# A two-layer transformer block in fp32: every remaining block of the modulation product moved into the first attention

## The chip, the cores and the metric

The kernel runs on one core of a Trainium2 chip, in one launch. The metric is the device time of that launch in microseconds (us). Three timed runs of the kernel before gave 3011.73, 3011.78 and 3012.26 us; the median is 3011.78.

## The reference

1024 latent tokens and 256 context tokens of width 1024 pass through two layers. Each layer has a mixer and a SwiGLU feed-forward network (FFN), each behind a normalisation that is modulated: shift, scale and gate come from one linear map of a conditioning vector.

```
for i in range(2):
    m_lat = silu(c)     @ ada_w[i] + ada_b[i]      # ada_w[i]: 1024 x 6144
    m_ctx = silu(c_ctx) @ ada_w[i] + ada_b[i]
    sh1, sc1, g1, sh2, sc2, g2 = split(m_lat, 6)    # the same for m_ctx
    h = rms(x, norm1_g[i]) * (1 + sc1) + sh1
    x = x + g1 * mixer_i(h, hc)                     # layer 0: Fourier groups and windowed attention
    h = rms(x, norm2_g[i]) * (1 + sc2) + sh2        # layer 1: neighbourhood attention
    x = x + g2 * ((silu(h @ wg) * (h @ wu)) @ wd)
    # layer 0 does the same for the context tokens
```

So the modulation of layer 1 depends on nothing but the inputs, and may be computed at any time before layer 1's first normalisation.

## The kernel before

All matrices are fp32. The large products run in three passes of a rounded 11-bit type (`mm3`, lines 74 to 76: high by high, low by high, high by low), so each weight tile is loaded raw, cast to its high part on ACT (line 774) and split to its low part on DVE (line 775) before TensorE (PE) can use it.

The stages follow each other in time. First come the first quarter of the modulation and layer 0's input projection, then the Fourier groups, and then layer 0's attention. After it come the output projection, layer 0's FFN (22 tiles of the hidden width, on 512, 256 and 512 tokens), layer 1's projection, its attention, and its FFN (22 tiles, on 512 and 512 tokens).

**The modulation product.** `ada_w` of both layers is cut into 48 blocks of 256 output columns, 1 MB each: blocks 0 to 23 are layer 0's, 24 to 47 layer 1's. `ada_block` (line 115) is a generator with three steps. Step 1 loads the block through SP's queue (line 124). Step 2, the products, is eight matmuls (line 130) that put the two conditioning vectors against 8 x 128 rows, in four groups of 32 output partitions, and a copy of the four partial rows on ACT (line 133, tile `ada_rows`, one buffer). Step 3, the sums, is two small matmuls against a 0/1 matrix `sel` (line 137) that add the four partial rows and turn them into columns, and an addition of the bias on DVE (line 138). Each of steps 2 and 3 takes one PSUM tile from the pool that the place of the call names.

The 48 blocks are spread over three places. Blocks 0 to 7 run at the very start. Blocks 8 to 23 run in layer 0's attention (lines 719 to 728). Blocks 24 to 47 run in layer 0's FFN: `modulation1` (line 1009) chains them, and `gate_up` (line 843) advances the chain by two steps behind the first chunk of tokens and by one behind each of the other two, from the third tile of the hidden width on (line 866). There the block is loaded in two halves of 512 KB into the ring `w_raw` (two buffers), the ring through which the FFN's own raw weights pass (line 772).

**Layer 0's attention.** It has 80 units (10 blocks of 128 queries, 2 key heads, 4 query heads), taken in 40 pairs by `pipeline2` (line 605). In each pair PE computes the scores of two new units (lines 602, 603), turns the probabilities of the pair two back (line 592, tiles `pt_ps`, three buffers) and multiplies older ones with the values (line 692, tile `po`). DVE adds the mask and takes the maximum (line 571) and copies turned tiles (line 598), ACT takes the exponents (line 577), POOL normalises (line 583). The calls in `before` are issued ahead of a pair's scores, those in `after` behind it. The order on PE, DVE, ACT and POOL is the written one here (`manual_schedule`); SP's order, and all orders in the FFN, are set by the scheduler of the framework. Every fourth pair starts with `load_q0` (line 642), which loads the next 128 queries (`qraw`, 512 KB) and turns them with eight matmuls (line 649) into two `pt_ps` tiles.

Of the kernel before, what the change touches and what calls it, by code (L numbers as in the profile page):

```python
# [9 lines left out]
F32 = mybir.dt.float32  # L10
# [6 lines left out]
P = 128  # L17
D = 1024
KT = D // P
# [36 lines left out]
def bc(ap, axis, n):  # L56

    ap = ap.unsqueeze(axis)
    shape = list(ap.shape)
    shape[axis] = n  # L60
    return ap.broadcast_to(shape)


def build(tc, io):
    nc = tc.nc
    V, S, G, TE = nc.vector, nc.scalar, nc.gpsimd, nc.tensor
    pools = Pools(tc)

    def fl(ap):
        return ap.bitcast(F32)  # L70
# [24 lines left out]
    csil = cst.tile([P, KT, 32], F32, name="csil")  # L95
# [16 lines left out]
    def vec(l, which):  # L112
        return mod[l][:, which * KT:(which + 1) * KT, :]

    def ada_block(b, xpool, wpool, ptr, name, parts=1, tag="x8"):

        l, ct = b // 24, 2 * (b % 24)  # L120
        n = KT // parts
        ws = [xpool.tile([P, n, 256], F32, name="ada_w", tag=tag) for _ in range(parts)]
        for i, w in enumerate(ws):
            nc.sync.dma_start(w, io["ada_w"][b, :, i * n:(i + 1) * n])
        yield
        ps = ptr.tile([P, 512], F32, name=name)
        for i in range(2):
            for q in range(4):
                k = 4 * i + q
                TE.matmul(ps[32 * q:32 * q + 32, :256], csil[:, k, :], ws[k // n][:, k % n],  # L130
                          start=i == 0, stop=i == 1, tile_position=(0, 32 * q))
        rows = wpool.tile([P, 256], F32, name="ada_rows", bufs=1)
        S.copy(rows, ps[:, :256])
        yield
        ps = ptr.tile([P, 512], F32, name=name)
        for j in range(2):
            TE.matmul(ps[:, 2 * j:2 * j + 2], rows[:, j * P:(j + 1) * P], sel, start=True, stop=True)
        V.tensor_tensor(mod[l][:, ct:ct + 2, :], ps[:, 0:4].rearrange("p (j m) -> p j m", j=2),
                        bc(adab[:, l, ct:ct + 2], 2, 2), ALU.add)

    def ada_gain(l, which, i, ks=slice(0, KT)):
        V.scalar_tensor_tensor(nA[i][:, ks], vec(l, which)[:, ks], 1.0, bc(ng[:, i, ks], 2, 2), ALU.add, ALU.mult)
# [10 lines left out]
    def advance(steps, n):  # L153

        for _ in range(n):
            if next(steps, steps) is steps:
                return
# [32 lines left out]
    x8, x8_cm = pools.open("x8", bufs=5)  # L190
# [161 lines left out]
    for c in range(T // CH):  # L352
        h_hi, h_lo = hs[c]

        for u in range(CH // P):
            j = c * (CH // P) + u
            if c == 0:
                pf, pq, _ = acc0[u]
# [7 lines left out]
            if j == NT - 1:  # L366
# [8 lines left out]
                first = butterfly(0, fp, 1)  # L375
# [56 lines left out]
    pst, pst_cm = pools.open("pst", bufs=2, psum=True)  # L432
# [42 lines left out]
    for half in range(2):  # L475
# [5 lines left out]
        for gg in range(2):  # L481
# [3 lines left out]
            for i0, parts in ((0, (0, 4)), (2, (1, 2)), (4, (3,))):  # L485
                ps = pA.tile([P, 2, 2, P], F32, name="ps_a")
# [7 lines left out]
                n = len(parts)  # L494
# [5 lines left out]
            for s0, n, sgn, l0, st in ((0, 2, 1, 0, 4), (2, 3, 1, 1, 1), (2, 3, -1, 7, -1)):  # L500
                ps = pB.tile([P, 4, P], F32, name="ps_b")
# [12 lines left out]
    g = fp.tile([P, 2, 512], F32, name="fg", tag="fa")  # L514
# [6 lines left out]
    for grp in range(4):  # L521
        ch = slice(grp * P, grp * P + P)
        a_hi, a_lo = a_parts(2)
        ps = pA.tile([P, 2, 2, P], F32, name="ps_a")
# [5 lines left out]
        ps = pB.tile([P, 4, P], F32, name="ps_b")  # L530
# [74 lines left out]
    def pipeline2(units, before, after):  # L605


        n = len(units) // 2
        last = max([n + 2] + [a + 1 for a in after])
        for b in range(last):  # L610
            new, old, turned = (units[2 * i:2 * i + 2] if 0 <= i < n else [] for i in (b, b - 1, b - 2))
            if b < n:
                for i in (2 * b, 2 * b + 1):
                    for f in before.get(i, ()):
                        f()
                    units[i] = units[i]()
                new = units[2 * b:2 * b + 2]
            for u in new:
                u.scores()
            for i in range(2):  # L620
                for u in old[i:i + 1]:
                    u.normalise()
                for u in new[i:i + 1]:
                    u.maxima()
                for u in turned[i:i + 1]:
                    u.turn()
                for u in new[i:i + 1]:
                    u.exponents()
            for f in after.get(b, ()):
                f()  # L630


    aw, aw_cm = pools.open("aw", bufs=2)
    xq, xq_cm = pools.open("xq", bufs=2)
    pss, pss_cm = pools.open("pss", bufs=2, psum=True)
    pst, pst_cm = pools.open("pst", bufs=3, psum=True)
    psv, psv_cm = pools.open("psv", bufs=1, psum=True)

    units, before, after = [], {}, {}
    qst = {}  # L640

    def load_q0(j):
        qraw = xq.tile([P, 1024], F32, name="qraw")
        nc.sync.dma_start(qraw, q_d[:, j, :])
        qst[j] = []
        for g in range(2):
            ps = pst.tile([P, 512], F32, name="pt_ps")
            for i in range(4):
                TE.transpose(ps[:, i * P:(i + 1) * P], qraw[:, (2 * i + g) * P:(2 * i + g + 1) * P], ident)
            q = aw.tile([P, 512], F32R, name=f"q{g}")  # L650
            S.copy(q, ps)
            qst[j].append(q)
# [63 lines left out]
            for e in range(2):  # L716
                group0(j, g, e)

    def modulation(ada, i):

        if i % 2 == 0 and i // 2 + 1 < len(ada):
            advance(ada[i // 2 + 1], 1)
        advance(ada[i // 2], 1 + i % 2)

    ada = [ada_block(b, xq, aw, pst, "pt_ps") for b in range(8, 24)]
    advance(ada[0], 1)
    for i in range(2 * len(ada)):
        before.setdefault(2 * (2 + i), []).append(lambda i=i: modulation(ada, i))
    with tc.manual_schedule(engines={E.PE, E.DVE, E.Activation, E.Pool}):
        pipeline2(units, before, after)  # L730
    ada_gain(0, 4, 1)
    pools.close(psv_cm, pst_cm, pss_cm, xq_cm, aw_cm, kv_cm, ac_cm)


    class Dense:
# [96 lines left out]
                yield  # L832
            lows.pop(0)()

        def ffn(self, first, last, tail=None, extra=iter(())):
            l, wk, tok, chunks = self.l, self.wk, self.tok, self.chunks
            act = {}

# [4 lines left out]
            def gate_up(f, chunks, side=iter(()), mid=lambda: None, mid2=lambda: None):  # L843
                if f not in act:
                    act[f] = open_act(f)
                ws, a_hi, a_lo = act[f]
                for c0, n, v in chunks:
                    sl = slice(c0, c0 + n)
                    g_ps = self.pg.tile([P, 512], F32, name="g_ps")
                    u_ps = self.pg.tile([P, 512], F32, name="u_ps")  # L850
                    for ps, w in zip((g_ps, u_ps), ws):
                        for k in range(KT):
                            mm3(ps[:, :n], w[0][:, k], w[1][:, k], self.h_hi[:, k, sl], self.h_lo[:, k, sl],
                                k == 0, k == KT - 1)
                            if ps is u_ps and k == 3:
                                mid2()
                        if ps is g_ps:
                            sg = wk.tile([P, 512], F32, name="sg", tag="t5")
                            S.activation(sg[:, :n], g_ps[:, :n], AF.Silu)  # L859
                            mid()  # L860
                    V.tensor_tensor(sg[:, :n], sg[:, :n], u_ps[:, :n], ALU.mult)  # L861
                    S.copy(a_hi[:, sl], sg[:, :n])  # L862
                    V.tensor_tensor(a_lo[:, sl], sg[:, :n], fl(a_hi[:, sl]), ALU.subtract)  # L863
                    advance(side, 8)
                    if f > 1:
                        advance(extra, 2 if c0 == 0 else 1)

            def down(fs, chunks, final=None, wd=None, own=iter(()), side=lambda dt: None):
                wd = wd or down_weights(fs)
# [42 lines left out]
            if not tail:  # L912
# [1 line left out]
                    gate_up(f, chunks)  # L914
                down(block, chunks, last)
                return
            advance(extra, 999)

            (cx, c0, c1), follow, side = tail

# [3 lines left out]
            f = block[-1]  # L924
# [25 lines left out]
    C0, C1, CX = (0, 512, 0), (512, 512, 0), (SEQ, CTX, 1)  # L950
# [4 lines left out]
    dl = Dense(0, T, (C0, CX, C1), o_hi, o_lo, x)  # L955
# [10 lines left out]
    steps, last = itertools.chain(*own), norm2(C1, lambda i: V)  # L966
# [39 lines left out]
        if dt in (2, 4):  # L1006
            w_first.append(w_in1(2, len(w_first), eng=G))

    def modulation1():
        for b in range(24, 48):  # L1010
            yield from ada_block(b, dl.wr, dl.wk, dl.pm, "pmisc", 2, "w_raw")
            yield
        ada_gain(1, 1, 2)
        ada_gain(1, 4, 3)

    steps = dl.ffn(last, fin0, ((CX, C0, C1), norm1, first_weights), modulation1())
    w_first += [w_in1(2, 2, eng=G), w_in1(2, 3, eng=G)]
    ctx_ps = [in_ps() for _ in range(2)]
    in_proj(w_first, (8, 9), range(2), ctx_ps)
# [30 lines left out]
    for i, cc in enumerate((2, 0, 4, 1, 3, 5)):  # L1050
        ws = w_first if cc == 2 else [w_in1(cc, kk, pool=w1 if i % 2 else dl.ww) for kk in range(4)]
        for j in ((8, 9) if cc >= 2 else ()) + tuple(range(8)):
            if cc == 2 and j >= 8:
                ps = ctx_ps[j - 8]
            else:
                ps = in_ps()
# [29 lines left out]
    aw, aw_cm = pools.open("aw1", bufs=2)  # L1086
    pss, pss_cm = pools.open("pss1", bufs=2, psum=True)
    pst, pst_cm = pools.open("pst1", bufs=3, psum=True)
# [7 lines left out]
    units, before, after = [], {}, {}  # L1096
# [128 lines left out]
    dl = Dense(1, SEQ, (C0, C1), h_hi, h_lo, x, by_col=True)  # L1225
    own = norm2(C0)
    dl.out_proj(io["w_out1"], (C0,), lambda dt: nc.sync.dma_start(x[:, dt], x_d[:, dt]), (own,))
    last = norm2(C1, lambda i: V)
# [120 lines left out]
```

## Time and profile before

The profiled execution took 3008.44 us, of which 3006.6 us is the span of its instructions.

| Quantity | Value |
|---|---|
| timed runs, median | 3011.78 us |
| profiled execution, time | 3008.44 us |
| its span | 3006.6 us |
| PE busy | 2889.4 us (96%) |
| DVE busy | 1381.9 us (46%) |
| ACT busy | 876.2 us (29%) |
| DMA, mean | 89 GB/s |
| granted clock of PE, mean | 0.983 |

"Busy" counts an instruction from start to end. Matmuls overlap in the array, so their starts say more than their durations: a 512-column matmul of the three-pass product is listed with 0.39 us but the next one starts 0.23 us after it. PEclk is the share of full clock that PE was granted. "Idle before" a row, in square brackets, names what released the engine.

The stages lie at 0 to 225 us (first modulation, projection), 225 to 237 (end of the Fourier groups), 237 to 406 (layer 0's attention), 406 to 560 (output projection, normalisation), 560 to 1450 (layer 0's FFN as far as modulation runs in it), 2300 to 2960 (most of layer 1's FFN).

### The profile page before, as it was taken

To read this page: it belongs to the slowest core of one execution; us is meant where nothing else is said; L and a number is where in the kernel's file an instruction comes from. 1 tells how busy PE (TensorE), PEld (TensorE's weight loads), DVE (VectorE), ACT (ScalarE), POOL (GpSimd) and SP (SyncE) were. 2 spreads that over 40 slices of the span, in tenths; PEclk is the share of its full clock that TensorE was granted. 3 is DMA by queue.
4 is the path that set the end of the run, shared out by engine and by line. 5 is a ranking of instruction groups with operands and counts; after the bars stand their busy time and mean duration, and the time that the engine had idled before them with its cause. 6 is when DMAs were issued, how large, how long until landed. Compare 5 with 4: busy or idle time off the path is not lost.

```text
span 3006.6 us, 38166 instructions
## 1 busy us (share of the span) xinstructions
PE 2889.4 (96%) x15290; PEld 2329.1 (77%) x15290; DVE 1381.9 (46%) x2530; ACT 876.2 (29%) x1672; POOL 313.2 (10%) x442
## 2 busy tenths in 40 slices
PE   7989999999999999999989999999999999999999
PEld 5877778877777877777876788777787888888887
DVE  5776646331313332233367334366664444444446
ACT  4346643211111111111145222466643111111110
POOL 0113321000000000000031000355310000000000
PEclk9999999999999999999999999999999999999999
DMA  7234342112121122121124433877331111111111
GB/s 271 86 113 169 120 141 79 35 49 70 50 71 69 57 71 71 43 70 56 57 74 130 121 104 103 200 174 177 119 112 49 43 49 43 56 43 50 49 43 70
DMA packets 120673, 267.19 MB, mean 89 GB/s; under 512 B 9616, under 2 KB 67472, under 8 KB 116528
## 3 DMA queue, kind: packets, MB, share of 16 engines
q1 hardware_dynamic: 114368, 247.89, 26.1%
q0 software_dynamic: 1952, 8.32, 1.0%
q10 hardware_dynamic: 4176, 8.53, 0.8%
q8 instruction: 121, 1.98, 0.3%
q14 instruction: 56, 0.46, 0.1%
HBM read 223.69 MB, written 41.03 MB: 88 GB/s over the span
## 4 chain that ended last, share of the span: by engine, by line
PE 88%; DVE 5%; DMA 3%; ACT 3%; issue 1%; POOL 1%; ACTq 0%; SPq 0%; POOLq 0%; DVEq 0%
PE d_ps L74 9%; PE d_ps L75 9%; PE d_ps L76 9%; PE g_ps L74 7%; PE g_ps L76 7%; PE g_ps L75 7%; PE u_ps L75 7%; PE u_ps L76 7%; PE u_ps L74 7%; PE pt_ps L592 3%; PE po L1177 3%; PE s_ps L602 2%; PE s_ps L603 2%; PE po L692 1%; DMA w_raw<-w_in 1%
## 5 line engine op out<-in xcount | busy, mean ns | idle before, releaser
L879 DVE SCALAR_TENSOR_TENSOR x<-d_ps,mod,x 128x512 f32<-128x512 f32 (+1 forms) x400 | 347.0, 880 | 164.1 <-PE d_ps L76 164.1
L861 DVE TENSOR_TENSOR sg<-sg,u_ps 128x512 f32<-128x512 f32 (+1 forms) x110 | 69.8, 634 | 694.0 <-PE u_ps L76 694.0
L774 ACT CAST w_hi<-w_raw 128x1024 fp32r<-128x1024 f32 x188 | 195.9, 1048 | 644.2 <-PE d_ps L75 328.5
L74 PE MATMUL d_ps<-act_hi,w_hi 128*128 128x512 f32 (+1 forms) x880 | 334.9, 381 | 19.0 <-ACT w_hi L774 15.6
L775 DVE TENSOR_TENSOR w_lo<-w_raw,w_hi 128x1024 fp32r<-128x1024 f32 x184 | 224.9, 1227 | 266.7 <-ACT w_hi L774 263.2
L75 PE MATMUL d_ps<-act_lo,w_hi 128*128 128x512 f32 (+1 forms) x880 | 333.4, 379 | 1.3 <-DVE act_lo L863 1.3
L76 PE MATMUL d_ps<-act_hi,w_lo 128*128 128x512 f32 (+1 forms) x880 | 327.3, 376 | 0.0
L74 PE MATMUL g_ps<-o_hi,w_hi 128*128 128x512 f32 (+1 forms) x528 | 196.6, 372 | 18.4 <-ACT w_hi L774 18.4
L74 PEld LDWEIGHTS d_ps<-act_hi,w_hi 128*128 128x128 f32 x880 | 169.0, 192 | 55.4 <-ACT w_hi L774 16.1
L75 PEld LDWEIGHTS d_ps<-act_lo,w_hi 128*128 128x128 f32 x880 | 169.2, 192 | 33.0 <-DVE act_lo L863 1.8
L76 PEld LDWEIGHTS d_ps<-act_hi,w_lo 128*128 128x128 f32 x880 | 168.4, 191 | 32.1
L75 PE MATMUL g_ps<-o_lo,w_hi 128*128 128x512 f32 (+1 forms) x528 | 193.2, 366 | 0.0
L76 PE MATMUL g_ps<-o_hi,w_lo 128*128 128x512 f32 (+1 forms) x528 | 192.5, 365 | 0.3 <-DVE w_lo L775 0.3
L859 ACT ACTIVATE sg<-g_ps 128x512 f32<-128x512 f32 (+1 forms) x110 | 61.0, 555 | 440.8 <-PE g_ps L76 440.0
L75 PE MATMUL u_ps<-o_lo,w_hi 128*128 128x512 f32 (+1 forms) x528 | 188.8, 358 | 0.0
L74 PE MATMUL u_ps<-o_hi,w_hi 128*128 128x512 f32 (+1 forms) x528 | 188.6, 357 | 0.0
L76 PE MATMUL u_ps<-o_hi,w_lo 128*128 128x512 f32 (+1 forms) x528 | 188.5, 357 | 0.0
L583 POOL TENSOR_SCALAR pr<-pr,st 128x640 f32<-128x640 f32 (+2 forms) x208 | 156.3, 752 | 225.3 <-DVE st L582 165.6
L862 ACT CAST act_hi<-sg 128x512 fp32r<-128x512 f32 (+1 forms) x110 | 63.5, 577 | 389.5 <-DVE sg L861 389.5
L577 ACT ACTIVATE pr<-sm,st 128x640 f32<-128x640 f32 (+4 forms) x208 | 162.7, 782 | 27.7 <-POOL sm L566 18.6
L809 POOL TENSOR_TENSOR nrm_ss<-nrm_ss,nrm_sq 128x512 f32<-128x512 f32 (+1 forms) x38 | 48.2, 1269 | 1169.6 <-PE d_ps L76 1046.6
L592 PE MATMUL pt_ps<-ident,pr 128*128 128x128 f32 x944 | 139.0, 278 | 6.8 <-ACT pt L596 3.5
(266 smaller groups left out, 6010.2 us busy)
## 6 DMA issues: line engine op xcount, KB each, us to landing
ada_w<-ada_w SPq DMA_DIRECT2D x24, 1024.0 KB, 4.9
ada_w<-ada_w SPq DMA_DIRECT2D x48, 512.0 KB, 4.0
w_raw<-w_gate SPq DMA_DIRECT2D x44, 512.0 KB, 3.2
w_raw<-w_up SPq DMA_DIRECT2D x44, 512.0 KB, 3.2
w_raw<-w_down SPq DMA_DIRECT2D x44, 512.0 KB, 3.3
k<-k_d SPq DMA_DIRECT2D x28, 640.0 KB, 10.1
w_raw<-w_out SPq DMA_DIRECT2D x32, 512.0 KB, 3.3
w_raw<-w_in SPq DMA_DIRECT2D x24, 512.0 KB, 4.1
```

What stands on the lines that cost most here:

```text
L74: TE.matmul(out, lh, rh, start=first, stop=False)
L75: TE.matmul(out, lh, rl, start=False, stop=False)
L76: TE.matmul(out, ll, rh, start=False, stop=last)
L577: S.activation(self.pr[:, :n], self.sm[:, :n], AF.Exp, bias=st[:, 0:1], scale=-1.0, accum_out=st[:, 1:2])
L583: G.tensor_scalar(self.pr[:, :n], self.pr[:, :n], st[:, 3:4], 0.0, ALU.mult, ALU.add)
L592: TE.transpose(pt[:, b * P:(b + 1) * P], self.pr[:, (b0 + b) * P:(b0 + b + 1) * P], ident)
L774: S.copy(hi, raw)
L775: eng.tensor_tensor(lo, raw, fl(hi), ALU.subtract)
L861: V.tensor_tensor(sg[:, :n], sg[:, :n], u_ps[:, :n], ALU.mult)
L862: S.copy(a_hi[:, sl], sg[:, :n])
L879: V.scalar_tensor_tensor(xs, self.shaped(ps[:, :n]), vec(l, 5)[:, dt, v:v + 1], xs, ALU.mult, ALU.add)
L1177: TE.matmul(po[64 * e_:64 * e_ + 64, us, :], d["v"][:, kt, 64 * e_:64 * e_ + 64], rhs(d["p", g, e_]), start=i == 0, stop=i == len(steps) - ...
```

## The change

All of blocks 8 to 47 run in layer 0's attention, one in each of the 40 pairs. Ahead of pair i the kernel issues the load of block i + 2, the products of block i and the sums of block i - 1 (counted from block 8). The loads of three blocks stand ahead of the first pair, and the last sums come behind the last pair. The pool for the blocks gets a third buffer (`ada_w`, 1 MB each), `qraw` keeps two. `modulation1` and the argument `extra` of the FFN are gone, and with them the halved blocks in the ring `w_raw`. The two gains of layer 1 (`ada_gain`, one DVE instruction each) are taken behind the attention.

```diff
-    def ada_block(b, xpool, wpool, ptr, name, parts=1, tag="x8"):
+    def ada_block(b, xpool, wpool, ptr, name):
         l, ct = b // 24, 2 * (b % 24)
-        n = KT // parts
-        ws = [xpool.tile([P, n, 256], F32, name="ada_w", tag=tag) for _ in range(parts)]
-        for i, w in enumerate(ws):
-            nc.sync.dma_start(w, io["ada_w"][b, :, i * n:(i + 1) * n])
+        w = xpool.tile([P, KT, 256], F32, name="ada_w", tag="x8")
+        nc.sync.dma_start(w, io["ada_w"][b])
         yield
...
-    xq, xq_cm = pools.open("xq", bufs=2)
+    xq, xq_cm = pools.open("xq", bufs=3)
...
-        qraw = xq.tile([P, 1024], F32, name="qraw")
+        qraw = xq.tile([P, 1024], F32, name="qraw", bufs=2)
...
-    def modulation(ada, i):
-
-        if i % 2 == 0 and i // 2 + 1 < len(ada):
-            advance(ada[i // 2 + 1], 1)
-        advance(ada[i // 2], 1 + i % 2)
-
-    ada = [ada_block(b, xq, aw, pst, "pt_ps") for b in range(8, 24)]
-    advance(ada[0], 1)
-    for i in range(2 * len(ada)):
-        before.setdefault(2 * (2 + i), []).append(lambda i=i: modulation(ada, i))
+    ada = [ada_block(b, xq, aw, pst, "pt_ps") for b in range(8, 48)]
+
+    def modulation(i):
+
+        for b, first in ((i + AHEAD, i == 0), (i, False), (i - 1, False)):
+            for g in ada[0 if first else max(b, 0):max(b + 1, 0)]:
+                advance(g, 1)
+
+    AHEAD = 2
+    for i in range(len(ada)):
+        before.setdefault(2 * i, []).append(lambda i=i: modulation(i))
+    after.setdefault(len(ada) - 1, []).append(lambda: modulation(len(ada)))
     with tc.manual_schedule(engines={E.PE, E.DVE, E.Activation, E.Pool}):
         pipeline2(units, before, after)
     ada_gain(0, 4, 1)
+    ada_gain(1, 1, 2)
+    ada_gain(1, 4, 3)
...
                     advance(side, 8)
-                    if f > 1:
-                        advance(extra, 2 if c0 == 0 else 1)
...
-            advance(extra, 999)
...
-    def modulation1():
-        for b in range(24, 48):
-            yield from ada_block(b, dl.wr, dl.wk, dl.pm, "pmisc", 2, "w_raw")
-            yield
-        ada_gain(1, 1, 2)
-        ada_gain(1, 4, 3)
-
-    steps = dl.ffn(last, fin0, ((CX, C0, C1), norm1, first_weights), modulation1())
+    steps = dl.ffn(last, fin0, ((CX, C0, C1), norm1, first_weights))
```

Three places of the program show what moves. In the rows, `x8` counts equal instructions, and "waits PE_49" says that the instruction waits for PE's semaphore; "DMAHW" are semaphores of earlier transfers. The changed kernel's line numbers are up to three lower (a load of weights is line 773 in place of 772, the products are line 127, the sums line 134).

**PE, in the middle of layer 0's attention.** Before, one pair has the products and the next one the sums:

```order
L592 MATMUL pt_ps<-ident,pr 128x128 x10
L692 MATMUL po<-pt,vt 64x256 x4
L130 MATMUL pt_ps<-ada_w,csil 32x256 x8
L602 MATMUL s_ps<-kB,q_2373 128x384
L603 MATMUL s_ps<-kLB,q_2373 128x384
```

```order
L592 MATMUL pt_ps<-ident,pr 128x128 x10
L692 MATMUL po<-pt,vt 64x256 x6
L137 MATMUL pt_ps<-sel,ada_rows 128x2 x2
L602 MATMUL s_ps<-kB,q_2373 128x384
L603 MATMUL s_ps<-kLB,q_2373 128x384
```

Now each pair has both:

```order
L589 MATMUL pt_ps<-ident,pr 128x128 x10
L689 MATMUL po<-pt,vt 64x256 x6
L127 MATMUL pt_ps<-ada_w,csil 32x256 x8
L134 MATMUL pt_ps<-sel,ada_rows 128x2 x2
L599 MATMUL s_ps<-kB,q_2426 128x384
L600 MATMUL s_ps<-kLB,q_2426 128x384
```

The products belong to block i and the sums behind them to block i - 1, and both stand ahead of the pair's scores.

**SP's queue, at the start of layer 0's attention.** Before, queries and blocks alternate:

```order
L644 DMA qraw<-q_d 128x1024 [waits DMAHW6_49,DVE_49,Pool_49]
L124 DMA ada_w<-ada_w 128x2048 [waits PE_49]
L644 DMA qraw<-q_d 128x1024 [waits DMAHW4_49]
L124 DMA ada_w<-ada_w 128x2048 [waits DVE_49,PE_49]
L644 DMA qraw<-q_d 128x1024 [waits DMAHW2_49,PE_49]
```

Now:

```order
L641 DMA qraw<-q_d 128x1024 [waits DMAHW6_49,DVE_49,Pool_49]
L122 DMA ada_w<-ada_w 128x2048 [waits PE_49]
L122 DMA ada_w<-ada_w 128x2048 [waits DMAHW4_49,DVE_49,PE_49]
L122 DMA ada_w<-ada_w 128x2048
L641 DMA qraw<-q_d 128x1024
L122 DMA ada_w<-ada_w 128x2048 [waits DMAHW7_49,DMAHW3_49,PE_49]
```

The second load of queries, which pair 1 needs, stands behind the second and the third block, and the second block waits for DVE and PE to be done with the memory that it takes over from the Fourier stage.

**SP's queue, at layer 0's FFN.** Before, the first blocks of layer 1's modulation stand between the FFN's weights:

```order
L124 DMA ada_w<-ada_w 128x1024 [waits DMAHW0_49,DVE_49]
L124 DMA ada_w<-ada_w 128x1024 [waits DMAHW1_49,DVE_49]
L124 DMA ada_w<-ada_w 128x1024 [waits DMAHW2_49,PE_49]
L124 DMA ada_w<-ada_w 128x1024 [waits DMAHW3_49,PE_49]
L772 DMA w_raw<-w_down 128x1024 [waits DMAHW4_49,PE_49]
L772 DMA w_raw<-w_down 128x1024 [waits DMAHW5_49,PE_49]
L772 DMA w_raw<-w_down 128x1024 [waits DMAHW6_49,DVE_49]
```

Now, at the same place of the FFN:

```order
L773 DMA w_raw<-w_gate 128x1024 [waits DMAHW6_49,DVE_49]
L773 DMA w_raw<-w_up 128x1024 [waits DMAHW7_49,DVE_49]
L773 DMA w_raw<-w_down 128x1024 [waits DMAHW0_49,DVE_49]
L773 DMA w_raw<-w_down 128x1024 [waits DMAHW1_49,DVE_49]
L773 DMA w_raw<-w_down 128x1024 [waits DMAHW2_49,DVE_49]
L773 DMA w_raw<-w_gate 128x1024 [waits DMAHW3_49,DVE_49]
```

Before, a load of weights behind a block waits for PE, which has to finish the products of that block before the buffer is free; now each load of weights waits for DVE alone, which has to finish the split of an earlier weight tile.

More of the change, by code (lines that the diff above doesn't have):

```diff
@@ L128, in ada_block @@
             for q in range(4):
-                k = 4 * i + q
-                TE.matmul(ps[32 * q:32 * q + 32, :256], csil[:, k, :], ws[k // n][:, k % n],
+                TE.matmul(ps[32 * q:32 * q + 32, :256], csil[:, 4 * i + q, :], w[:, 4 * i + q],
                           start=i == 0, stop=i == 1, tile_position=(0, 32 * q))
@@ L833, in norm, with ffn @@
             lows.pop(0)()
-        def ffn(self, first, last, tail=None, extra=iter(())):
+        def ffn(self, first, last, tail=None):
             l, wk, tok, chunks = self.l, self.wk, self.tok, self.chunks
```

## The prediction

> **What bounds the kernel now.** I read the page first (the chain that ended last), then the table of stages, then PE's waits in the stage that loses something, then its rows in order of time.
>
> ```profile
> PE 88%; DVE 5%; DMA 3%; ACT 3%; issue 1%; POOL 1%; ACTq 0%; SPq 0%; POOLq 0%; DVEq 0%
> ```
>
> PE holds 88% of the chain that ended last, so a change is worth what it does to PE's time line. The stages (from:to, length, busy time of each engine with its count, granted clock, DMA share, GB/s) show where that line has holes:
>
> ```profile
> core 0: us, PE busy (x) PEld busy (x) DVE busy (x) ACT busy (x) POOL busy (x), PEclk, DMA share, GB/s
> 237.00:406.00 169.00, 163.36 (x1357) 118.72 (x1355) 112.01 (x358) 106.55 (x282) 67.32 (x158) 1.00 0.38 133
> ...
> 560.00:1450.00 890.00, 846.43 (x4470) 695.73 (x4469) 264.45 (x389) 127.92 (x194) 0.00 (x0) 0.96 0.18 63
> ...
> 2300.00:2960.00 660.00, 660.00 (x2834) 531.21 (x2833) 294.49 (x282) 106.85 (x138) 0.00 (x0) 1.00 0.14 47
> ```
>
> Layer 1's FFN, which has no modulation in it, keeps PE busy for 660.00 of 660.00 us at full clock. Layer 0's FFN, with 24 blocks of modulation in it, leaves PE idle for 890 - 846.43 = 43.6 us and gets a mean clock of 0.96. PE's waits in that stage (what waited <- what ended it: us in total, times, longest) name the cause:
>
> ```profile
> PE g_ps L74 <- ACT w_hi L774: 18.4, 6, 3.2
> PE d_ps L74 <- ACT w_hi L774: 15.6, 6, 2.6
> PE pmisc L137 <- ACT ada_rows L133: 9.2, 12, 0.8
> PE g_ps L76 <- DVE w_lo L775: 0.3, 1, 0.3
> ```
>
> Twelve waits for a block's own copy (sums directly behind products), and twelve for the cast of a weight tile. One such place in order of time, PE's rows first, then SP's:
>
> ```profile
> 609.97 0.40 PE L75 MATMUL u_ps<-o_lo,w_hi 128*128 128x512 f32 x1
> 610.20 0.39 PE L76 MATMUL u_ps<-o_hi,w_lo 128*128 128x512 f32 x1
> 610.52 1.07 PE L130 MATMUL pmisc<-ada_w,csil 128*32 128x256 f32 x16
> 612.36 0.61 PE L137 MATMUL pmisc<-sel,ada_rows 128*128 128x2 f32 x4 [0.77 <-ACT ada_rows L133]
> 615.60 0.79 PE L74 MATMUL d_ps<-act_hi,w_hi 128*128 128x512 f32 x1 [2.62 <-ACT w_hi L774]
> 616.19 0.63 PE L75 MATMUL d_ps<-act_lo,w_hi 128*128 128x512 f32 x1
> 616.61 0.63 PE L74 MATMUL d_ps<-act_hi,w_hi 128*128 128x512 f32 x1
> ...
> 620.88 0.91 PE L76 MATMUL d_ps<-act_hi,w_lo 128*128 128x512 f32 x3
> ```
>
> ```profile
> 611.22 0.81 SPq L772 DMA_DIRECT2D w_raw<-w_down  x2
> ```
>
> The weights that PE needs at 611 are only asked for at 611.22: their raw buffer held the modulation block until its products had run. PE then waits for transfer and cast until 615.60, and its next matmuls start 0.42 us apart (616.19 to 616.61) in place of 0.23 (609.97 to 610.20), until about 621: the clock was cut in half. The other twelve blocks fall where nothing is late:
>
> ```profile
> 592.22 1.07 PE L130 MATMUL pmisc<-ada_w,csil 128*32 128x256 f32 x16
> 593.22 0.39 PE L74 MATMUL g_ps<-o_hi,w_hi 128*128 128x256 f32 x1
> ...
> 598.80 0.50 PE L137 MATMUL pmisc<-sel,ada_rows 128*128 128x2 f32 x4
> 599.16 0.48 PE L74 MATMUL g_ps<-o_hi,w_hi 128*128 128x512 f32 x1
> ```
>
> There a block costs its own slots, 593.22 - 592.22 = 1.00 us for the products and 0.36 us for the sums.
>
> **What the change removes.** All of this leaves layer 0's FFN. First the holes, 18.4 + 15.6 + 9.2 + 0.3 = 43.5 us. Second the slots, 24 x (1.00 + 0.36) = 32.6 us. Third the slow clock, 846.43 x (1 - 0.96) = 33.9 us; the clock has two digits, so 29.6 to 38.1. Sum 110.0 us, bounds 106 to 114. The same sum another way: over all PE rows from 592 to 1450, how much later each next start came than its undisturbed distance, the modulation's rows in full, adds up to 111.4 us, in twelve places of 6.6 to 8.4 us like the first one shown and twelve of 1.5 to 1.8 us like the second. What would make this smaller is a load that is late for its own reasons; layer 1's FFN, with the same ring, loads and casts and less PE time for each weight (two chunks of tokens in place of three), has no idle time, so I count zero.
>
> The clock's share is where a rule can be held against the trace. The rows above show half spacing from 615.60 to about 621, 5 us. The Trainium skill, page "TensorE: Matmul & The Clock Gate", section on the HAM clock gate, says that the clock drops to half after an idle window of about 3.4 us and returns after a busy one of the same length. By that the twelve long places would lose at most 12 x 1.7 = 20 us in place of 33.9, and the time would come out 14 us higher; the trace differs, since its slow stretch is longer than one window, and the sum goes by the trace.
>
> **What it adds in the attention.** PE's rows there, and the most frequent wait of its weight loads for a block's products:
>
> ```profile
> 308.61 0.51 PE L137 MATMUL pt_ps<-sel,ada_rows 128*128 128x2 f32 x4
> 308.98 0.42 PE L602 MATMUL s_ps<-kA,q 128*128 128x384 f32 x1
> ...
> 312.57 1.07 PE L130 MATMUL pt_ps<-ada_w,csil 128*32 128x256 f32 x16
> 313.57 0.44 PE L602 MATMUL s_ps<-kB,q 128*128 128x384 f32 x1
> ```
>
> ```profile
> PEld pt_ps L130 <- DVE st L571: 5.0, 13, 0.4
> ```
>
> A block takes 1.00 + 0.37 = 1.37 us of PE, with no wait ahead of it. PE is busy for 163.36 of 169 us in this stage, so nothing hides them: 24 x 1.37 = 32.9 us. Lower bound 27.3, if all 5.6 us of idle time took them in. Upper bound 52, if each of the 48 added steps also met a wait of 0.4 us, as the weight loads show (hidden behind running matmuls now). I take 32.9, the rows' own distance. ACT's copy `ada_rows` now also waits for the sums behind the products, since `ada_rows` has one buffer; behind it in ACT's queue stands the copy of a turned tile, which PE produces only after the scores, so nobody waits. DVE's addition comes behind the products too, and behind it stands the reciprocal whose result POOL needs for the next pair only.
>
> **The start of the attention.** The second load of queries now stands behind two blocks. SP's queue, PE's rows at pair 1, and what transfers take in 225 to 250 us (count, size, us to landing):
>
> ```profile
> 225.64 0.43 SPq L644 DMA_DIRECT2D qraw<-q_d  x1
> 234.83 0.33 SPq L124 DMA_DIRECT2D ada_w<-ada_w  x1
> ```
>
> ```profile
> 236.47 1.03 PE L649 MATMUL pt_ps<-ident,qraw 128*128 128x128 f32 x8
> 237.75 0.39 PE L602 MATMUL s_ps<-kA,q 128*128 128x256 f32 x1 [0.24 <-ACT q L651]
> ...
> 238.79 1.04 PE L649 MATMUL pt_ps<-ident,qraw 128*128 128x128 f32 x8
> ```
>
> ```profile
> GB/s 0 26 131 223 419 433 426 367 400 118 0 0 0 0 0 0 0 144 118 419 459 413 334 400 229 0 0 0 157 79 406 419 419 361 419 256 26 0 144 131
> ...
> qraw<-q_d SPq DMA_DIRECT2D x3, 512.0 KB, 5.6
> ```
>
> Before, the queries of pair 1 were asked for at 225.64, 13 us ahead. Now they come behind a block that waits until 234.83 and a second one, so at about 235.6. Before they took 5.6 us to land; the load at 225.64 had one block ahead of it, and another MB at the 419 GB/s of the busy slices adds 2.5 us: landed at 243.7. PE wants them at 238.79 plus block 8's products (1.00 us, of which 0.5 falls into the wait for q at 237.75), 239.3. That is a hole of 4.4 us, and behind it the clock may fall as in the FFN (33.9 / 12 = 2.8 us each). Bounds 0 (the transfers interleave kindly) and 7.2; I take 6, nearer to the second, because both parts have rows.
>
> **The end of it.** Six of the last pairs had no step of modulation and wait for DVE; the added slots fill a part of that. The raw weights of the output projection, asked for at 378.63 before, now follow the last block.
>
> ```profile
> 395.93 0.65 PE L692 MATMUL po<-pt,vt 128*64 128x256 f32 x4 [0.80 <-DVE o_lo L700]
> ...
> 406.25 0.80 PE L74 MATMUL d_ps<-o_hi,w_hi 128*128 128x512 f32 x1 [1.42 <-ACT w_hi L774]
> ```
>
> ```profile
> 378.63 0.81 SPq L772 DMA_DIRECT2D w_raw<-w_out  x2
> ```
>
> ```profile
> w_raw<-w_out SPq DMA_DIRECT2D x32, 512.0 KB, 3.3
> ```
>
> I take -1.5 us for the first (the 0.80 here, and smaller ones). For the second nothing: the last products end some 8 us before the matmul at 406.25, a load of 512 KB lands in 3.3 us, and ACT casts only after its last output tile. If that cover failed it would cost up to 3 us.
>
> **Sum.** 3008.44 - 110.0 + 32.9 + 6 - 1.5 = 2935.8 us for a profiled execution. This one was 3.3 us below the median of the timed runs, so I forecast 2939 us.
>
> **The rivals.**
> 1. The three `pt_ps` buffers bind. Each pair now takes two of them ahead of its four turned tiles, and a wait for ACT's or DVE's eviction enters PE's line twice a pair. For it: these waits exist for PE's weight loads, 0.4 us at most. Against it: they are hidden behind the running matmuls now. Price: 40 x 2 x 0.4 = 32 us, so 2971.
> 2. The FFN's holes stay, because weights are late without the modulation too. Only slots and the 9.2 us of copies go: 3011.8 - 41.8 + 37.4 = 3007, 0.15% faster. Against it stands layer 1's FFN with no idle time.
> 3. The blocks come too slowly (the other side). Attention now moves 40 x 1.05 + 10 x 0.52 = 47 MB. If DMA gave no more than the 133 GB/s of this stage, it would last 355 us in place of 169 + 33, and the kernel 2939 + 153 = 3092. It turns slower when the rate stays below 47 MB in 169 + 110 us, 169 GB/s. Against it: 1 MB each 5 us is 210 GB/s, and the busy slices show twice that; a block is asked for nearly three pairs before its products.
>
> **Chances.** Forecast 0.79, with a range of its own of 2928 to 2956; rival 1 0.10, rival 2 0.05, rival 3 0.03, something else 0.03. Range for 8 in 10: the low end takes the lower bounds together (3011.8 - 114 + 27.3 = 2925), the high end stops a little short of rival 1: 2925 to 2962. A measurement of this kernel tells 0.2% (6 us) from no change. Faster by more than that: 0.94; within it, from rival 2: 0.03; slower, from rival 3: 0.03.
>
> **What would show it.** Right: layer 0's FFN has no PE wait for `w_hi`, a clock of 1.00 and is 110 us shorter; the attention is some 37 us longer, PE still busy in it, with one hole of 3 to 5 us near its start at the turning of the second queries. Wrong: waits of PE for `ada_w` in every pair (rival 3) or for ACT and DVE copies of `pt_ps` (rival 1), or `w_hi` still named in the FFN (rival 2).

## The result, and the profile after

| Quantity | Before | Changed |
|---|---|---|
| timed runs, median | 3011.76 us (3010.94 to 3012.26, 4 runs) | 2940.72 us (2938.65 to 2941.68, 4 runs) |
| ratio, 95% interval | | 0.9763 [0.9747, 0.978] |
| profiled execution, its span | 3008.44 us, 3006.6 us | 2940.7 us, 2938.9 us |
| granted clock, mean | 0.983 | 0.993 |

The forecast was 2939 us, and the time lies 1.7 us above it. The stages show where it went (from:to, length, busy time of PE and the other engines, granted clock, DMA share, GB/s). First layer 0's attention, from the turning of the first queries to the first matmul of the output projection, in the kernel before:

```profile
236.47:406.25 169.78, 163.89 (x1362) 119.25 (x1361) 112.03 (x359) 107.13 (x283) 67.32 (x158) 1.00 0.39 134
```

The same stretch in the changed kernel, and its layer 0's FFN:

```profile
237.56:448.89 211.33, 201.84 (x1842) 141.28 (x1840) 115.16 (x385) 116.57 (x307) 67.15 (x158) 0.98 0.64 230
...
597.00:1378.00 781.00, 781.00 (x4017) 660.87 (x4016) 260.20 (x362) 117.31 (x171) 0.00 (x0) 1.00 0.11 39
```

The attention is 211.33 - 169.78 = 41.6 us longer. The FFN's stage is 781 us in place of 890, without an idle moment and at full clock. The first matmul of that FFN starts at 521.9 us before and at 564.5 us now, so from there to the end of the span it is 3006.6 - 521.9 = 2484.7 against 2938.9 - 564.5 = 2374.4 us: 110.3 us less (112.1 by a second profile of the changed kernel). The twelve waits for `w_hi` and the twelve for `ada_rows` have left PE's list for the FFN; what remains between 500 and 1400 us is

```profile
PE pmisc L170 <- DVE nrm_v L84: 0.9, 1, 0.9
```

In the attention PE has one wait worth the name, and it is at the start. PE's waits there, PE's rows and SP's rows:

```profile
PE pt_ps L646 <- DMA qraw<-q_d: 5.9, 1, 5.9
PE po L689 <- DVE o_lo L697: 0.8, 1, 0.8
```

```profile
246.63 1.94 PE L646 MATMUL pt_ps<-ident,qraw 128*128 128x128 f32 x8 [5.92 <-DMA qraw<-q_d]
248.50 1.94 PE L127 MATMUL pt_ps<-ada_w,csil 128*32 128x256 f32 x16
...
252.08 1.07 PE L127 MATMUL pt_ps<-ada_w,csil 128*32 128x256 f32 x16
```

```profile
237.76 0.81 SPq L122 DMA_DIRECT2D ada_w<-ada_w  x2
238.61 0.43 SPq L641 DMA_DIRECT2D qraw<-q_d  x1
```

The second queries are asked for at 238.61 us, behind two blocks that SP issued from 237.76 us on, and PE stands still for 5.92 us until they are there. Behind the hole the eight products of a block take 1.94 us where they take 1.07 a little later: the granted clock is 0.50 from 243.84 to 250.67 us, so for the first 4.0 us after the hole, which by the rows loses about 1.9 us more. Further on a pair of units pays for its block as in these rows of the changed kernel:

```profile
302.55 1.07 PE L127 MATMUL pt_ps<-ada_w,csil 128*32 128x256 f32 x16
303.55 0.61 PE L134 MATMUL pt_ps<-sel,ada_rows 128*128 128x2 f32 x4
304.02 0.42 PE L599 MATMUL s_ps<-kA,q 128*128 128x384 f32 x1
```

That is 304.02 - 302.55 = 1.47 us for products and sums.

### The profile page after: what moved, and what is told of

Read it like the earlier page. It is cut to its first block, busy times and chain, and to the rows that moved or that the text cites. A ratio compares the mean times of both kernels' runs of the same rounds, so it can differ in the third digit from the quotient of the medians.

```text
span 2938.9 us, 38168 instructions
## 1 busy us (share of the span) xinstructions
PE 2860.1 (97%) x15290; PEld 2316.5 (79%) x15290; DVE 1381.5 (47%) x2530; ACT 875.5 (30%) x1672; POOL 313.6 (11%) x442
## 5 line engine op out<-in xcount | busy, mean ns | idle before, releaser
L74 PE MATMUL d_ps<-act_hi,w_hi 128*128 128x512 f32 (+1 forms) x880 | 328.0, 373 | 3.4 <-DVE x L878 3.4
L74 PEld LDWEIGHTS d_ps<-act_hi,w_hi 128*128 128x128 f32 x880 | 165.7, 188 | 37.4 <-DVE x L878 5.6
L74 PE MATMUL g_ps<-o_hi,w_hi 128*128 128x512 f32 (+1 forms) x528 | 188.5, 357 | 0.0
L75 PE MATMUL g_ps<-h_lo,w_hi 128*128 128x512 f32 x352 | 139.6, 397 | 1.0 <-DVE h_lo L829 1.0
```

The costliest lines, as they stand in the source:

```text
L74: TE.matmul(out, lh, rh, start=first, stop=False)
L75: TE.matmul(out, lh, rl, start=False, stop=False)
```

## What the experiments asked

The forecast came out, but a sum can be right with wrong terms. Three questions stayed. Was it the blocks' place in the ring of the raw weights that made the FFN's holes, or their work? Is a block in the attention worth its PE time and nothing else? Can the hole at the start be had back? The comparisons below of one FFN place with another are made over all rows of the three-pass matmuls between 560 and 1460 us: how much later each next start came than 0.233 us (512 columns) or 0.1145 us (256), the distances of undisturbed rows. The kernel before has twelve long places of 6.9 to 8.5 us, 92 us together, and twelve short ones of 1.64 us.

### The FFN without the loads, and with the loads alone

The first kernel leaves out the loads of blocks 24 to 47:

```diff
+        if parts == 1:
+            ws = [xpool.tile([P, n, 256], F32, name="ada_w", tag=tag) for _ in range(parts)]
+            for i, w in enumerate(ws):
+                nc.sync.dma_start(w, io["ada_w"][b, :, i * n:(i + 1) * n])
...
+                out, src = ps[32 * q:32 * q + 32, :256], bc(ident, 1, 2)
+                if parts == 1:
+                    src = ws[k // n][:, k % n]
```

> The kernel before, with the loads of blocks 24 to 47 left out of layer 0's FFN: their products read the identity instead, so that 192 products of four passes each, their copies, sums and advances stay where they were and only the 48 halves in the ring of the raw weights are gone (layer 1's modulation is then wrong). Theory (the holes in the FFN are the down weights waiting for slots of that ring, which the blocks hold): the waits for the down weights' high parts (18.4 + 15.6 us) go and with them most of the 33.9 us of slow clock, while the slots of products and sums and the 9.2 us of waits for ScalarE's copy stay: 3008 - 34 - 30, about 2944 us (2938 to 2955), and the clock of the FFN's stage near 1.00. Rival (the holes come from the products and sums themselves, or from engines that the sums delay): within 5 us of before, about 3007 us.

Measured 2939.61 us (2935.08 to 2941.7), 0.9761 [0.9744, 0.9777] of the kernel before, 71.6 us less. The FFN's stage, cut at the same times as in the prediction:

```profile
560.00:1450.00 890.00, 890.00 (x4852) 738.77 (x4851) 289.57 (x427) 133.77 (x208) 0.00 (x0) 1.00 0.11 37
```

PE is busy for 890.00 of 890 us at full clock, with all the products and sums still in it. All 24 places are now short, 1.63 to 1.68 us each. The rival falls. The time is some 4 us below the theory's figure, and PE's list of waits for this stretch is empty: the 9.2 us of waits for ScalarE's copy went too, though copies and sums are still there.

The second kernel keeps the loads and drops the work:

```diff
+        if parts > 1:
+            ps = ptr.tile([P, 512], F32, name=name)
+            for w in ws:
+                TE.matmul(ps[0:32, 0:2], csil[:, 0, :], w[:, 0, 0:2], start=True, stop=True)
+            yield
+            V.memset(mod[l][:, ct:ct + 2, :], 0.0)
+            return
```

> The kernel before, with only the loads of blocks 24 to 47 left in layer 0's FFN: both halves of each block still come through the ring of the raw weights and are read by one matmul of two columns each, but the products and sums are left out and the modulation of layer 1 is set to zero by VectorE (so it is wrong). Theory (ring sharing): the holes at the down weights and the slow clock behind them stay, the 24 slots of 1.36 us and the 9.2 us of waits for ScalarE's copy go: 3008 - 33 - 9, about 2967 us (2960 to 2980), with the FFN's clock still near 0.94. Rival (products and sums make the holes): the FFN loses all of its 110 us, about 2900 to 2935 us.

Measured 3001.72 us (2999.72 to 3004.47), 0.9972 [0.9961, 0.9983]: 9.5 us less, where the theory had 42 and the rival 75 or more. Both missed, and the waits tell why. PE's waits in the FFN, the same place as in the prediction, and the chain behind it on SP and ScalarE:

```profile
PE g_ps L74 <- ACT w_hi L781: 29.0, 6, 5.1
PE d_ps L74 <- ACT w_hi L781: 29.0, 6, 5.1
```

```profile
611.87 0.29 PE L129 MATMUL pmisc<-ada_w,csil 128*32 128x2 f32 x4
616.85 0.79 PE L74 MATMUL d_ps<-act_hi,w_hi 128*128 128x512 f32 x1 [4.70 <-ACT w_hi L781]
```

```profile
612.12 6.29 SPq L779 DMA_DIRECT2D w_raw<-w_down  x3
...
615.76 1.04 ACT L781 CAST w_hi<-w_raw 128x1024 fp32r<-128x1024 f32 x1 [2.37 <-DMA w_raw<-w_down]
```

The waits for the weights' high parts grew from 34.0 to 58.0 us. From the block's first product (611.87) to the weight's first matmul (616.85) it takes 4.98 us: issue, landing, cast. In the kernel before it takes 615.60 - 610.52 = 5.08 us, and inside these lie the block's products, the 0.77 us wait for the copy and the sums. So at the twelve long places slots and copy waits cost nothing: they fill a time that the ring sets. Without them the places stay as long (7.1 to 8.7 us, 95 us together, 3 more than before). Only the short ones fall, from 1.64 to 0.41 us each, which with a new wait of 1.3 us elsewhere makes 12 to 13 us. Less the 3, that is 9 to 10 us, against 9.5 measured.

### The same loads, the same ring, another order

If the ring's order is the cause, it can be mended in the FFN itself. A block has three steps, load, products, sums; a group of weights (one tile of the hidden width) has three chunks of tokens, and the kernel before advances the blocks by four steps in each. So of four blocks two have their load behind the second or the last chunk of a group, and their products at the end of the group or later. Such a block stands in the ring ahead of the next weights, and its products have to run before these can be loaded: PE's rows have products and sums together directly ahead of the waiting matmul, at twelve of 24 blocks. One line gives each block a whole group (and five groups two blocks):

```diff
-                        advance(extra, 2 if c0 == 0 else 1)
+                        advance(extra, ((1, 1, 1), (2, 3, 1))[f < 7][(0, SEQ, 512).index(c0)])
```

> The kernel before, with only the steps of the blocks counted out differently in layer 0's FFN: load, products and sums of a block all fall between two groups of weights (one step behind each of the three chunks; in five groups two blocks), so that no block's load stands in the ring ahead of the next group's or the down weights while its products are still to come. Loads, ring, slots and copies stay, and the whole is computed. Theory now (the 12 long places are the ring's order: products, landing, cast and the waiting matmul in a chain of about 5 us, in which the block's own slots and the copy's wait lie hidden; the 12 short places cost 1.65 us each): all 24 places become short, 90 - 12 x 1.65 = 70 us less, about 2939 us (2935 to 2945), with no waits for the weights' high parts and the clock at 1.00. Rival (the 24 MB of blocks do not go through a ring of two beside the weights, in whatever order): most of the 34 us of waits stays, 2960 us or more.

Measured 2937.58 us (2936.6 to 2938.18), 0.976 [0.9747, 0.9773] of the kernel before. One line in place of the whole move gives the same time. The FFN's stage, PE's only wait in it (560 to 1460 us) and SP's largest wait:

```profile
560.00:1450.00 890.00, 890.00 (x4861) 740.21 (x4860) 291.76 (x429) 138.79 (x209) 0.00 (x0) 1.00 0.20 66
```

```profile
PE pmisc L167 <- POOL nrm_ss L809: 0.8, 1, 0.8
```

```profile
SPq L772 <- PE pmisc L130: 430.6, 19, 42.5
```

In the kernel before that last row reads

```profile
SPq L772 <- PE pmisc L130: 405.6, 18, 45.5
```

The loads of weights wait as long for the products as before, 25 us longer even, and nothing is lost by it. (With the loads of the blocks themselves, SP's waits for products are 498.5 us in place of 543.7.) What counts is whether PE needs what stands behind the waiting load within the next 5 us or one chunk later (512 tokens take 48 x 0.233 = 11.2 us).

### The attention without the products, and without the loads

Both start from the changed kernel. The first leaves out products and sums of layer 1's blocks.

```diff
+        if l:
+            ps = ptr.tile([P, 512], F32, name=name)
+            TE.matmul(ps[0:32, 0:2], csil[:, 0, :], w[:, 0, 0:2], start=True, stop=True)
+            yield
+            V.memset(mod[l][:, ct:ct + 2, :], 0.0)
+            return
```

> The changed kernel, with the 24 blocks of layer 1 loaded in the attention as they are, but their products and sums left out: one matmul of two columns reads each block, and VectorE sets layer 1's modulation to zero (so it is wrong). Theory (TensorE is the bound of the attention, and a block there costs its slot of about 1.37 us and nothing else): 24 x 1.37 = 33 us less, about 2908 us (2902 to 2915), from the attention's stage alone. Rival (the attention is held by its 40 MB of blocks or by the vector engines, and the products lie in time that is idle anyway): no change, about 2940 us.

Measured 2913.88 us (2907.85 to 2914.79), 0.9673 [0.9659, 0.9688]. The attention, and one slot that is left:

```profile
235.63:418.16 182.53, 171.73 (x1410) 123.67 (x1408) 110.35 (x385) 108.02 (x283) 67.17 (x158) 0.98 0.74 266
```

```profile
332.10 0.22 PE L126 MATMUL pt_ps<-ada_w,csil 128*32 128x2 f32 x2
332.25 0.44 PE L605 MATMUL s_ps<-kB,q 128*128 128x384 f32 x1
```

The attention is 211.33 - 182.53 = 28.8 us shorter. The remaining matmul takes 0.15 us, so 24 x (1.47 - 0.15) = 31.7 us of PE's time should have gone. Its busy time in the stage fell by 201.84 - 171.73 = 30.1 us, and its idle time grew from 9.5 to 10.8 us. The median fell by 27 us. That lies in the expected range, but the theory had 33: it did not count the small matmul (24 x 0.15 = 3.6 us). The last 2 us can't be told from what profiles differ by: from the first matmul of layer 0's FFN to the end of the span, which the edit leaves as it is, it takes 2374.4 and 2372.6 us in two profiles of the changed kernel and 2378.1 us here. A block costs its slot, within 2 to 3 us of 32; the rival falls.

The second leaves out the loads.

```diff
-        w = xpool.tile([P, KT, 256], F32, name="ada_w", tag="x8")
-        nc.sync.dma_start(w, io["ada_w"][b])
+        if l == 0:
+            w = xpool.tile([P, KT, 256], F32, name="ada_w", tag="x8")
+            nc.sync.dma_start(w, io["ada_w"][b])
...
+                out, src = ps[32 * q:32 * q + 32, :256], bc(ident, 1, 2)
+                if l == 0:
+                    src = w[:, 4 * i + q]
```

> The changed kernel, with the loads of layer 1's 24 blocks left out: their products read the identity instead and everything else stays (layer 1's modulation is then wrong). Theory (the loads are covered, the products on TensorE are what costs): no change, 2941 us within 2. Rival (24 MB more on the DMA queues slow something else in the attention, its key and query transfers or the weights of the next stage): several us less, 2925 to 2936 us.

Measured 2940.73 us (2939.89 to 2941.52), 0.9767 [0.9752, 0.9781], equal to the changed kernel. The attention:

```profile
237.26:448.50 211.24, 201.96 (x1843) 141.38 (x1841) 115.18 (x385) 116.63 (x307) 67.16 (x158) 0.98 0.31 111
```

211.24 us with 111 GB/s, against 211.33 with 230: the transfers of 24 MB are fully covered.

### The sums directly behind their own products

```diff
-        for b, first in ((i + AHEAD, i == 0), (i, False), (i - 1, False)):
+        for b, first in ((i + AHEAD, i == 0), (i, False), (i, False)):
```

> The changed kernel, with the sums of each block directly behind its own products, in the same slot, instead of a slot later; the whole is computed. Theory (TensorE works in order, and between products and sums lies ScalarE's copy of the rows, for which the kernel before waited 0.77 us each time that sums followed products directly): 40 waits of 0.8 us or, with ScalarE busy with the softmax, more: 31 to 60 us, about 2975 us (2965 to 3000). Rival (the copy is hidden, and the pair's distance is worth nothing in the attention): within 3 us of 2941.

Measured 2967.74 us (2966.37 to 2968.43), 0.9858 [0.9845, 0.9872], 27 us more than the changed kernel. PE's waits in the attention:

```profile
PE pt_ps L134 <- ACT ada_rows L130: 24.0, 40, 1.5
```

Forty waits of 0.6 us, 24.0 us, and the attention is 239.69 us long, 28.4 more. So the distance of a pair between products and sums is worth 27 us here; without it the change would stand at 0.9858 in place of 0.9763. The wait was 0.6 us and not the 0.8 expected; the time fell into the range.

### The start: queries first, blocks later

```diff
+    def fetch_q0(j):
+        qst["raw", j] = xq.tile([P, 1024], F32, name="qraw", bufs=2)
+        nc.sync.dma_start(qst["raw", j], q_d[:, j, :])
...
+    fetch_q0(order[0])
+    fetch_q0(order[1])
...
+        if i + 2 < NT:
+            before[len(units) + 2].append(lambda j=order[i + 2]: fetch_q0(j))
```

> The changed kernel, with one thing moved: the transfer of each pair's queries is put into SP's queue one pair earlier, so that the queries of the second pair stand ahead of the first blocks of the attention instead of behind two of them; nothing else changes, and the whole is computed. Theory (the 5.9 us hole and the about 2 us of half clock behind it come from the queries' place in the queue): both go, about 2933 us (2931 to 2936). Rival (the second queries are late because their buffer or the whole queue comes free late, or the blocks that now land later make a hole of the same size): within 2 us of 2941.

Measured 2934.63 us (2929.9 to 2936.59), 0.9744 [0.9731, 0.9758]. The start on PE:

```profile
237.38 1.04 PE L649 MATMUL pt_ps<-ident,qraw 128*128 128x128 f32 x8
...
240.40 1.03 PE L649 MATMUL pt_ps<-ident,qraw 128*128 128x128 f32 x8
242.56 1.07 PE L127 MATMUL pt_ps<-ada_w,csil 128*32 128x256 f32 x16 [1.12 <-ACT pr L574]
```

The hole is gone, and with it the half clock; a wait of 1.12 us comes in its place. The attention is 204.62 us long, 6.7 less. Since a few microseconds may also lie between two chips, it ran once more beside the changed kernel:

> The changed kernel with the queries' transfers queued one pair earlier, once more, beside the changed kernel on the same chip; the whole is computed. Theory (the queries' place in the queue made the start's hole, 5.9 us and about 2 us of half clock, of which 1.1 us came back as another wait): 5 to 7 us below the changed kernel. Rival (the difference between the two was one of chips): within 2 us of it.

> The changed kernel itself, as a measure for the two beside it on the same chip: 2941 us within 3, and its start with the 6 us hole at the turning of the second queries.

Measured 2934.60 us (2931.61 to 2936.4), 0.9748 [0.9735, 0.9761], against 2939.06 us (2936.74 to 2940.56), 0.9763 [0.975, 0.9777]. Queries first is 4.5 us faster, 0.15%, a little less than the 5 to 7 us of the theory and more than the 2 us of the rival. The timed runs of the two don't overlap, the intervals of the ratios do; what carries it is the profile, which has the attention 6.7 us shorter both times. Of the versions that compute the whole it has the lowest median.

One slot of lead in place of two, alone and with the queries first:

```diff
-    AHEAD = 2
+    AHEAD = 1
```

> The changed kernel, with each block put into SP's queue one slot ahead of its products instead of two; the ring of three buffers stays, and the whole is computed. Theory (SP runs ahead of TensorE and only the ring holds it, so a block's load starts when the product three blocks before it is done, whatever the slot it is queued in): no waits for blocks appear, and since one block less stands ahead of the second queries the hole at the start shrinks by the 2.5 us that a block takes to come, about 2938 us (2936 to 2941). Rival (the two slots of lead are needed: a slot is about 5.1 us and a block lands 4.8 us after its issue): waits for blocks of 0.5 us and more on most of 40, 2960 us or more.

> The changed kernel with both edits: queries queued one pair earlier, blocks one slot ahead instead of two; the whole is computed. Theory: as with the queries moved alone, about 2933 us (2931 to 2937), since the hole has one cause. Rival (the two edits remove different waits): 2 us or more below the better of the two.

Measured 2937.83 us (2934.83 to 2941.38) and 2938.1 us (2934.28 to 2941.02), both 0.976 of the kernel before. Alone, the hole shrinks as expected, from 5.92 to 3.29 us, and no wait for a block appears:

```profile
243.21 1.84 PE L646 MATMUL pt_ps<-ident,qraw 128*128 128x128 f32 x8 [3.29 <-DMA qraw<-q_d]
```

So in the middle of the attention the lead in the program is worth nothing: SP runs ahead, and the ring of three buffers sets when a load starts. With both edits the median is 3.5 us above that of the queries first alone, which neither theory had. The ranges of the two overlap, and the two profiled executions took about the same (2934.28 and 2934.93 us), so no difference of the whole is shown. What the profiles do show is the attention: 444.6 - 235.84 = 208.8 us in place of 204.6. PE's waits, the two rows that wait and the stages of the start, with both edits:

```profile
PE pt_ps L127 <- DMA ada_w<-ada_w: 2.3, 2, 1.3
```

```profile
240.91 1.07 PE L127 MATMUL pt_ps<-ada_w,csil 128*32 128x256 f32 x16 [1.02 <-DMA ada_w<-ada_w]
...
244.82 1.59 PE L127 MATMUL pt_ps<-ada_w,csil 128*32 128x256 f32 x16 [1.25 <-DMA ada_w<-ada_w]
```

```profile
240.00:245.00 5.00, 2.84 (x32) 2.14 (x36) 1.73 (x9) 3.18 (x10) 1.65 (x4) 1.00 1.01 419
245.00:251.00 6.00, 6.00 (x40) 4.75 (x36) 1.83 (x7) 2.37 (x7) 1.07 (x3) 0.52 0.99 407
```

With queries first alone:

```profile
240.00:245.00 5.00, 3.88 (x41) 3.14 (x39) 1.88 (x7) 2.85 (x7) 0.46 (x1) 1.00 1.00 419
245.00:251.00 6.00, 5.97 (x64) 4.27 (x64) 3.98 (x16) 4.43 (x12) 2.96 (x9) 1.00 1.02 427
```

Two waits for a block, 2.3 us together, leave PE busy for 2.84 of 5 us, and the granted clock is 0.50 from 245.23 to 252.06 us, with PE at work all the time: about 3 us lost.

## Why the prediction was right, and where it was not

**The FFN, 110.0 us.** Right as a sum (110.3), and right in that both the holes and the slow clock come with the blocks: PE's waits for `w_hi` are gone and the clock is 1.00. Rival 2, weights late of their own, fell with the kernel without the loads, whose FFN is busy throughout. The working failed in the step that priced holes, slots and clock as three terms of their own. The runs show two that don't add like that: the loads in the ring are worth 71.6 us when they alone go, and the slots are worth 24 x 1.65 = 39.6 us, but only once the holes are gone; with the holes there, work and copy waits together are worth 9.5 us. The price of a slot was 1.36 us in the prediction, the sum of two row distances; by all rows it is 1.65, as the matmuls around a switch start late too, so 39.6 us in place of 32.6. The slow clock was put at 33.9 us; behind the twelve waits the rows of the kernel before start 27.8 us late in all. The product of busy time and clock took in stretches of half clock in which PE stood still, as at 614.17 to 615.60 us. These two errors, 7.0 and 6.1 us, cancel, so that the sum of terms came within 0.3 us is luck. The second way of summing that the prediction gave, late starts by place (111.4 us), was the sounder one, since it doesn't ask which of two overlapping causes holds the time.

**What the FFN's holes were.** The prediction had the ring as the cause, and that holds. What it had not seen is that the holes hung on the order of the steps, not on the FFN as a place: with one line changed there, the time is that of the changed kernel.

**The attention, 32.9 us.** The step was "1.00 + 0.37 = 1.37 us of PE" for a block. It measured 1.47, since sums behind products take 0.47 (303.55 to 304.02). For all 40 blocks: 24 x 1.47 + 16 x 0.10 = 36.9 us.

**The start, 6 us.** The mechanism was right, the size 2 us short: 5.92 + 1.9 = 7.8 us. The step that failed is the time at which the second block's buffer comes free. The prediction took the row of the kernel before, 234.83; now SP waits longer, for a DVE instruction of the stage ahead, and issues at 237.76:

```profile
SPq L122 <- DVE a_lo L526: 10.1, 1, 10.1
```

PE could then start on the queries 8.0 us after their issue (238.61 to 246.6), close to the 5.6 + 2.5 us assumed.

**The end, -1.5 us.** PE's idle time in the attention was 169.78 - 163.89 = 5.9 us before and 211.33 - 201.84 = 9.5 now, of which 5.9 is the hole: the added slots filled 2.3 us of old waits. 36.9 + 7.8 - 2.3 = 42.4 us, against 41.6 measured and 37.4 predicted.

**The offset of 3.3 us.** The sum for a profiled execution was 2935.8 us; the profiled one took 2940.7, 4.9 us more: 4.2 from the attention, 1.1 because the attention begins at 237.56 in place of 236.47, and 0.3 the other way from the FFN. In the profiles of all these kernels, which share their first stage, it begins between 235.34 and 240.33, in the changed kernel's second profile at 237.81, so this 1.1 can't be told from what runs differ by. The 3.3 us that were added for the median were not there this time (2940.7 profiled, 2940.72 median). The two errors nearly cancel; that the forecast lies 1.7 us off, and not 5, is luck.

**Rivals 1 and 3.** No wait of PE for a copy out of `pt_ps` beyond 0.2 us, and DMA moved 230 GB/s in the attention; without the new loads its length is the same.

**The clock's rule.** The prediction set a rule of the Trainium skill, page "TensorE: Matmul & The Clock Gate", section on the HAM clock gate (half clock after an idle window of about 3.4 us, back after a busy one), against 33.9 us in the FFN. The trace bears out its last part at the start of the attention, where the granted clock was back at 1.00 at 250.67 us, after 3.41 us that PE filled. The prediction held against the rule that the slow stretch in the FFN was longer than one window. That does not follow: the granted clock was 0.50 there from 614.17 to 621.00 us, which is twice 3.41 us, and PE stood still up to 615.60 us and filled the second half alone. With queries first and one slot of lead, though, half clock went on behind 3.42 us that PE filled (245.23 to 248.65). The trace differs on what starts it: the longest wait in the FFN before was 3.2 us, and with queries first and one slot of lead no wait was longer than 1.3 us and the half clock lasted 6.8 us.

## What to carry to other kernels

When loads for two purposes share a ring, look at which load stands behind one whose reader comes later in the program: the chain from that reader over issue, landing and cast (5 us here) lands on the engine that needs the second load, and moving the steps by a chunk can be worth as much as moving the work elsewhere. Work that lies inside such a chain costs nothing until the chain is gone, so don't add the price of the holes to the price of the work in them without a run or a sum over late starts. Before a transfer is queued ahead of others, ask which one is needed first: two blocks ahead of one load of queries cost 7.8 us, and putting the queries first took 4.5 us off the time.

## What was not expected of the hardware

The granted clock falls without one long idle stretch. With queries first and one slot of lead there were two waits of 1.02 and 1.25 us. PE was busy for 2.15 of the 3.41 us up to 245.23 us, and the next 6.83 us had half clock. With queries first alone and one wait of 1.12 us, PE was busy for 2.30 of 3.42 us (240.04 to 243.46), and the clock stayed at 1.00. The two are close, so these runs give no threshold. In the kernel before, half clock came with each of the twelve waits of 2.6 to 3.2 us and lasted 3.41 us (five times) or 6.83 us (seven times). These waits, 34.0 us together, had 27.8 us of late starts behind them. Short waits can thus cost about as much again as they last, though not every one does.
